# Four small edits to an encoder layer on one core: the attention planner's score cost, one copy's engine, the waits of the x rows, and the engine of one weight sum

## The chip, the cores and the metric

The kernel runs on one core of a Trainium2 chip. The metric is the device time of one execution in microseconds (us), from the first to the last instruction and what the launch adds around them.

## What is computed

One layer for 1024 prompt frames and 64 frames of a running stream: a half-step SwiGLU, two token mixers side by side (differential attention and retention) merged by gates, a second half-step SwiGLU, and a final norm. All of it is float32.

```python
x = x + 0.5 * g1 * swiglu(modulate(rms_norm(x, norm_f1), sh1, sc1), w_up1, w_down1)
hm = modulate(rms_norm(x, norm_mix), shm, scm)
q_a, k_a, v_a, q_r, k_r, v_r, z_r, gate_a, gate_r = split(hm @ w_in)
o_a = diff_attention(q_a, k_all, v_all)            # two softmaxes per head, a = p0 - lam * p1
o_r, s_new = retention(rotary(q_r), rotary(k_r), v_r, state)
o_a = head_rms_norm(o_a, da_norm) * (1 - lam_init)
o_r = head_group_norm(o_r, ret_norm) * silu(z_r)
merged = sigmoid(gate_a) * (o_a @ w_a_proj) + sigmoid(gate_r) * (o_r @ w_r_proj)
x = x + gm * (merged @ w_o)
x = x + 0.5 * g2 * swiglu(modulate(rms_norm(x, norm_f2), sh2, sc2), w_up2, w_down2)
y = rms_norm(x, norm_final)                        # shifts, scales and gates come from silu(c) @ w_ada + b_ada
```

The prompt's queries see earlier chunks of the prompt. The stream's 64 queries see a cache of 2048 keys and themselves.

## The kernel before

The 1088 columns (frames) are worked in two halves, g=0 (512 columns) and g=1 (576, the stream's 64 among them). Large products of a pair of weight blocks use a Strassen-like scheme (`pair_weights`, `products`, lines 520 to 554): seven products instead of eight. Each product is four blocks of three matmuls (`mm3`, lines 159 to 164), because every float32 operand is split into a high and a low part (`split`, line 132): ScalarE casts the high part (line 134), and VectorE or GpSimd subtracts it to get the low part (line 138).

For each pair of weight blocks `pair_weights` loads two raw tiles and makes four sums s1 to s4 (`add`, line 518). s2 needs s1, and s4 needs s2. Then it splits three tiles of sums and raw weights and one smaller one. `LOE` and `SE` say which engine makes each low part and each sum; `phase(i)` picks a row of them for each stage. Row 1 is that of the mixers. There are three buffers for such halves (NW = 3), so the weights of the next pair are made while the products of this one give buffers back.

The stages in order:

- First SwiGLU (`ffn`, line 565), g=0 then g=1. Beside the products of `up`, a side generator is advanced by a fixed number of steps (`pump`). At the start it runs `side_work` (line 808), which interleaves, by the string `PAT`, steps of the adaLN product (`ada`, "g"), yields ("y") and steps of `load_x(1, later)` ("r"). `load_x` takes g=1's x rows in five tiles: it issues a load into a single buffer, yields `WAIT` times, transposes the tile on TensorE, copies it with VectorE and ScalarE, and yields once more.
- Mixers (from line 859). Sums of squares of the last half (`sqa[1]`) are copied to another pool (line 862) for the norm of the next stage (lines 342 to 346). Then each half runs 20 pairs of products of w_in, that is 140 products. After each product `tick(g)` (line 968) gives the other tasks (attention, the stream's decode attention, retention) a budget of 2.0, of which each step takes its stated cost; a step yields its delay and its cost. `att_core` (line 1087) states the cost of a score step as 0.0034 x 128 for each block of 128 keys. When the pairs are done, the remaining tasks are run to their end (line 1399).
- Merge of the mixers (`project`, `add_out`), and the second SwiGLU with the final norm.

The order of instructions on each engine is then fixed by the compiling framework, which follows the program order and takes what it thinks is ready. At run time each engine is in order.

Of the kernel before, what the change touches and what calls it, by code (L numbers as in the profile page):

```python
# [34 lines left out]
DA, DB, DH, DR, DT, DX = 4, 1, 4, 2, 2, 2  # L35
UA = 12
DC, DK, DV, EARLY = 2, 2, 1, True
# [3 lines left out]
NB = len(BLK)  # L41
GRP = [(0, 512), (512, 576)]
BGRP = [[0, 1], [3, 2]]
NY, NV, NTT, SIDE0, SIDE, TAIL, SLACK, NRA, NS0, WAIT, NNEAR = 4, 2, 6, 7, 3, 2, 5, 3, 3, 1, 2
LOP = (1, 4)
NDG = 4
PAT = "gyry" * 8 + "g"
# [36 lines left out]
def encoder_layer(tc: tile.TileContext, a, o, stage=9):  # L84
    nc = tc.nc
# [10 lines left out]
    def close(*names):  # L96
        for name in names:
            guards.pop(name).__exit__(None, None, None)
# [27 lines left out]
    def misc():  # L126
        return psum["pool"].tile([P, 512], F32, tag="misc", name="misc", bufs=psum["misc"])
# [38 lines left out]
    V, G = nc.vector, nc.gpsimd  # L166
    LOE, SE = [], []
    LOES = [[G, V, V, V, G], [G, V, G, V, V], [G, V, V, G, G]]
    SES = [[G, G, G, G], [G, V, G, G], [V, V, G, G]]
    FE = [[V, V, G, G], [G, G, G, G], [V, V, V, G], [V, V, G, G]]  # L170

    def phase(i):
        LOE[:], SE[:] = LOES[i], SES[i]

# [659 lines left out]
    sqa = {}  # L834
# [24 lines left out]
    phase(1)  # L859
    upool = pool("u")  # L860
    sq1 = upool.tile([P, 576], F32, tag="ft", name="sq1", bufs=NFT)
    nc.vector.tensor_copy(sq1, sqa[1])
    close("n1", "x1", "ps_f1", "acc")
    mpool = pool("mix", "right")
    spsum = pool("ps_mix", space=PSUM)
# [19 lines left out]
    def c4():  # L885
        return dec["pool"].tile([P, dec["c4"]], F32, tag="c4", name="c4", bufs=NC4)

    def small(n=P):
        return mpool.tile([P, n], F32, tag=f"s{n}", name="s", bufs=6 if n == P else 4 if n > P else 2)

    def col(n=1):
        return mpool.tile([P, 8], F32, tag="col", name="col", bufs=24)[:, :n]
# [4 lines left out]
    def st():  # L897

        return dec["ps"].tile([P, dec["st"]], F32, tag="S", name="S", bufs=2048 // dec["st"])
# [65 lines left out]
    def spawn(gen, delay=1):  # L965
        tasks.append([now[0] + delay, gen])
# [103 lines left out]
    def heads_out(rows, ss, n, w, dcols, dst):  # L1070

        f = rsqrt(ss[:w, :n], 1.0 / VD)
        for j in range(n):
            nc.scalar.mul(rows[:, j], rows[:, j], f[:w, j:j + 1])
        yield DH, 0.1
        ot = c4()
        t = misc()
        for j in range(4):
            nc.tensor.transpose(t[:, j * w:(j + 1) * w], rows[:, j], ident[:w, :w])
        for j in range(0, 4, 1 if len(dcols) > 1 else 4):  # L1080
            e = (j + 1 if len(dcols) > 1 else 4) * w
            nc.scalar.mul(ot[:, j * w:e], t[:, j * w:e], dcols[j % len(dcols)])
        for q, (d, a0, a1) in enumerate(dst):
            nc.sync.dma_start(d, ot[:, a0:a1])
        yield 1, 0.9

    def att_core(g, h, q, ks, v, done):

        rows, ss = [], col(8)

        def scores(r):
            w = P * (4 * g + r + 1)
            p, sums = [], col(2)
            t = st()
            half = dec["st"] // 2
            both = t[:, :half], t[:, half:]
            for k, k0 in ks:
                k1 = min(k0 + 512, w)
                for c, s in enumerate(both):
                    cs = slice(c * HD, (c + 1) * HD)  # L1100
                    nc.tensor.matmul(s[:, k0:k1], q[cs, r * P:(r + 1) * P], k[cs, :k1 - k0], start=True, stop=True)
            for c, s in enumerate(both):
                nc.vector.memset(s[:HD, w - HD:w], -1e30)
                nm, sm = col(), sums[:, c:c + 1]
                nc.vector.tensor_reduce(out=nm, in_=s[:, :w], op=ALU.max, axis=AX.X, negate=True)
                e = c4()
                nc.scalar.activation(e[:, :w], s[:, :w], AF.Exp, bias=nm, accum_out=sm)
                p.append(e)
            rs, cf = col(2), col()
            nc.vector.reciprocal(rs, sums)  # L1110
            r0, r1 = rs[:, 0:1], rs[:, 1:2]
            nc.vector.scalar_tensor_tensor(out=cf, in0=sums[:, 0:1], scalar=r1, in1=neglam, op0=ALU.mult, op1=ALU.mult)
            nc.vector.scalar_tensor_tensor(out=p[0][:, :w], in0=p[1][:, :w], scalar=cf, in1=p[0][:, :w],
                                           op0=ALU.mult, op1=ALU.add)
            return p, r0

        def values(r, at, r0):
            if not rows:
                rows.append(mpool.tile([P, 4, P], F32, tag="rows", name="rows", bufs=1))
            n = 4 * g + r + 1  # L1120
            t = misc()
            for j in range(n):
                nc.tensor.matmul(t[:, :P], at[:, j * P:(j + 1) * P], v[j], start=(j == 0), stop=(j == n - 1))
            nc.scalar.mul(rows[0][:, r], t[:, :P], r0)
            nc.scalar.activation(small(), t[:, :P], AF.Square, scale=r0, accum_out=ss[:, r:r + 1])
            return 0.22 * n

        p, r0 = scores(0)
        yield DA, 0.0034 * 128 * (4 * g + 1)
        for r in range(4):  # L1130
            i = 4 * g + r
            at = p[1]
            for j0 in range(0, i + 1, 4):
                t = misc()
                n = min(4, i + 1 - j0)
                for j in range(n):
                    nc.tensor.transpose(t[:, j * P:(j + 1) * P], p[0][:, (j0 + j) * P:(j0 + j + 1) * P], ident)
                nc.scalar.copy(at[:, j0 * P:(j0 + n) * P], t[:, :n * P])
            yield DB, 0.22 * (i + 1)
            cur = r, at, r0  # L1140
            if r < 3 and EARLY:
                p, r0 = scores(r + 1)
                if r == 2:
                    done()
                yield DC, 0.0034 * 128 * (i + 2)
            cost = values(*cur)
            if r < 3 and not EARLY:
                p, r0 = scores(r + 1)
                if r == 2:
                    done()  # L1150
                cost += 0.0034 * 128 * (i + 2)
            yield DA - (DC if EARLY else 0), cost
        spawn(heads_out(rows[0], ss, 4, P, [dcol[:, h:h + 1]], [(osp_a[h][:, g * 512:g * 512 + 512], 0, 512)]))

# [183 lines left out]
    for g in range(2):  # L1338
# [9 lines left out]
        def attend():  # L1348
            for h in range(HEADS):
                yield from until(("q", h), ("v", h))  # L1350
                ks, vs = [(got["k", h], 512 * g)], [got["v", h][:, j] for j in range(4)]
                if g:
                    ks.insert(0, (kv(ksp[h]), 0))
                    va = kv(vsp[h]).rearrange("p (j c) -> p j c", c=P)
                    vs = [va[:, j] for j in range(4)] + vs
                    yield 3, 0.1
                yield from att_core(g, h, got["q", h], ks, vs, lambda: free("q", h))
                free("v", h)
# [25 lines left out]
        while lins or rest:  # L1384
            if lins and live[0] + lins[0][0] <= dec["u"]:
                n, f, i = lins.popleft()
# [120 lines left out]
    sqa = npool.tile([P, 576], F32, tag="yf", name="sqa", bufs=NY)  # L1507
# [97 lines left out]
```

## Time and profile before

| what | us |
|---|---|
| median of three runs | 2578.6 (2573.17 to 2580.3) |
| profiled execution, its own time | 2576.09 |
| its span, first to last instruction | 2574.3 |
| TensorE (PE) busy | 2446.7 (95%) |
| VectorE (DVE) busy | 1818.7 (71%) |
| GpSimd (POOL) busy | 1618.6 (63%) |
| ScalarE (ACT) busy | 1125.2 (44%) |

A busy PE is not always a PE at full speed: its matmuls overlap, and the granted clock falls at times. Stretches of the span have to be read one by one. Where PE sits idle, the view of waits says which instruction on which engine released it; that instruction may be late because its own engine, which is in order, was held by something else.

### The profile page before, as it was taken

To read this page: it belongs to the slowest core of one execution; us is meant where nothing else is said; L and a number is where in the kernel's file an instruction comes from. 1 tells how busy PE (TensorE), PEld (TensorE's weight loads), DVE (VectorE), ACT (ScalarE), POOL (GpSimd) and SP (SyncE) were. 2 spreads that over 40 slices of the span, in tenths; PEclk is the share of its full clock that TensorE was granted. 3 is DMA by queue.
4 is the path that set the end of the run, shared out by engine and by line. 5 is a ranking of instruction groups with operands and counts; after the bars stand their busy time and mean duration, and the time that the engine had idled before them with its cause. 6 is when DMAs were issued, how large, how long until landed. Compare 5 with 4: busy or idle time off the path is not lost. (4 is left out here: it accounts for less than half of the span.)

```text
span 2574.3 us, 45302 instructions
## 1 busy us (share of the span) xinstructions
PE 2446.7 (95%) x17278; PEld 2259.9 (88%) x17278; DVE 1818.7 (71%) x3132; ACT 1125.2 (44%) x1928; POOL 1618.6 (63%) x1058
## 2 busy tenths in 40 slices
PE   6999999999999889998999998999999999999998
PEld 3888889999999778887878986798889998999998
DVE  5586667776666897787665664557877777766766
ACT  4443335443334445553445545534444444333333
POOL 5796676887666466686444533655767665756562
PEclk9999999999999999999999998999999999999999
DMA  8655445554443553543333336646453335323331
GB/s 284 218 189 157 141 153 194 176 152 146 140 137 102 179 172 117 170 154 113 109 110 104 117 98 203 197 130 220 122 166 106 99 101 185 112 91 91 91 91 38
DMA packets 425005, 365.25 MB, mean 142 GB/s; under 512 B 18780, under 2 KB 358420, under 8 KB 424788
## 3 DMA queue, kind: packets, MB, share of 16 engines
q1 hardware_dynamic: 424608, 362.28, 45.3%
q8 instruction: 137, 2.24, 0.4%
q14 instruction: 80, 0.66, 0.1%
q10 hardware_dynamic: 180, 0.06, 0.0%
HBM read 307.95 MB, written 52.10 MB: 140 GB/s over the span
## 5 line engine op out<-in xcount | busy, mean ns | idle before, releaser
L162 PE MATMUL misc<-h,whi 128*128 128x288 f32 (+2 forms) x3360 | 1010.8, 301 | 32.8 <-DVE t L518 15.8
L164 PE MATMUL misc<-h,wlo 128*128 128x288 f32 (+2 forms) x3360 | 988.7, 295 | 9.7 <-DVE wlo L138 6.7
L163 PE MATMUL misc<-h,whi 128*128 128x288 f32 (+2 forms) x3360 | 990.0, 295 | 5.1 <-DVE h L138 5.0
L162 PEld LDWEIGHTS misc<-h,whi 128*128 128x128 f32 x3360 | 645.7, 192 | 72.4 <-DVE t L518 18.5
L164 PEld LDWEIGHTS misc<-h,wlo 128*128 128x128 f32 x3360 | 645.6, 192 | 16.4 <-DVE wlo L138 8.1
L163 PEld LDWEIGHTS misc<-h,whi 128*128 128x128 f32 x3360 | 645.8, 192 | 14.9 <-DVE h L138 7.1
L138 POOL TENSOR_TENSOR wlo<-raw,whi 128x1024 fp32r<-128x1024 f32 x150 | 374.7, 2498 | 270.3 <-ACT whi L134 236.2
L518 DVE TENSOR_TENSOR t<-misc,t 128x256 f32<-128x256 f32 (+1 forms) x560 | 235.0, 432 | 235.0 <-PE misc L164 202.0
L138 DVE TENSOR_TENSOR wlo<-ws,whi 128x1024 fp32r<-128x1024 f32 x178 | 313.5, 1761 | 62.4 <-ACT whi L134 61.1
L138 POOL TENSOR_TENSOR wd<-raw,wd 128x512 fp32r<-128x512 f32 x176 | 233.6, 1349 | 100.5 <-ACT wd L134 100.4
L653 DVE SCALAR_TENSOR_TENSOR x<-misc,gate,x 128x288 f32<-128x288 f32 (+3 forms) x540 | 239.8, 486 | 52.5 <-PE misc L164 45.1
L134 ACT CAST whi<-ws 128x1024 fp32r<-128x1024 f32 x178 | 186.7, 1049 | 203.6 <-PE misc L163 125.7
L134 ACT CAST whi<-raw 128x1024 fp32r<-128x1024 f32 x160 | 167.4, 1046 | 215.3 <-PE misc L163 170.8
L518 POOL TENSOR_TENSOR ws<-raw 128x512 f32<-128x512 f32 x134 | 192.4, 1438 | 98.9 <-DVE wlo L138 60.6
L134 ACT CAST wd<-raw 128x512 fp32r<-128x512 f32 x176 | 102.7, 619 | 186.9 <-PE misc L164 172.0
L162 PE MATMUL misc<-h,wd 128*128 128x288 f32 (+3 forms) x552 | 178.8, 327 | 5.1 <-DVE t L518 3.1
L163 PE MATMUL misc<-h,wd 128*128 128x288 f32 (+3 forms) x552 | 178.6, 325 | 0.0
L164 PE MATMUL misc<-h,wd 128*128 128x288 f32 (+3 forms) x552 | 176.4, 324 | 0.0
L518 POOL TENSOR_TENSOR h<-raw 128x512 f32<-128x512 f32 x78 | 109.7, 1407 | 84.1 <-issue 34.5
L162 PE MATMUL misc<-h,wb 128*128 128x256 f32 (+1 forms) x512 | 151.5, 296 | 5.2 <-ACT h L134 4.2
L163 PE MATMUL misc<-h,wb 128*128 128x256 f32 (+1 forms) x512 | 148.9, 291 | 0.0
L164 PE MATMUL misc<-h,wb 128*128 128x256 f32 (+1 forms) x512 | 148.9, 291 | 0.0
(297 smaller groups left out, 4787.2 us busy)
## 6 DMA issues: line engine op xcount, KB each, us to landing
raw<-in_w_up_dram SPq DMA_DIRECT2D x176, 512.0 KB, 4.0
raw<-in_w_down_dram SPq DMA_DIRECT2D x88, 512.0 KB, 4.0
raw<-in_w_in_dram SPq DMA_DIRECT2D x80, 512.0 KB, 4.0
rawa<-in_w_ada_dram SPq DMA_DIRECT2D x24, 1024.0 KB, 6.6
h<-in_w_ada_dram SPq DMA_DIRECT2D x16, 512.0 KB, 7.0
raw<-in_w_o_dram SPq DMA_DIRECT2D x16, 512.0 KB, 4.3
raw<-far SPq DMA_DIRECT2D x14, 576.0 KB, 3.7
yf<-xsp SPq DMA_DIRECT2D x24, 288.0 KB, 4.3
```

What stands on the lines that cost most here:

```text
L134: nc.scalar.copy(hi, src)
L138: eng.tensor_tensor(out=lo, in0=src, in1=hi.bitcast(F32), op=ALU.subtract)
L162: nc.tensor.matmul(out, wh, xh, start=first, stop=False)
L163: nc.tensor.matmul(out, wh, xl, start=False, stop=False)
L164: nc.tensor.matmul(out, wl, xh, start=False, stop=last)
L518: eng.tensor_tensor(out=out, in0=in0, in1=in1, op=op)
L653: nc.vector.scalar_tensor_tensor(out=xm, in0=t[:, c0 - cs.start:c1 - cs.start], scalar=gate()[:, m, s:s + 1], in1=xm, op0=ALU.mult, op1=AL ...
```

## The change

Four edits:

- `att_core` states the cost of a score step as 0.0018 x 128 for each block of 128 keys, in place of 0.0034 x 128, at all three places.
- The copy of the sums of squares (line 862) is made by ScalarE in place of VectorE.
- `WAIT` is 2 in place of 1: a yield more between the load of a tile of g=1's x rows and its transposes.
- In the mixers' row of `SES` the second of the four weight sums, s2 = s1 - a1, is made by GpSimd in place of VectorE, so that GpSimd makes all four.

```diff
-NY, NV, NTT, SIDE0, SIDE, TAIL, SLACK, NRA, NS0, WAIT, NNEAR = 4, 2, 6, 7, 3, 2, 5, 3, 3, 1, 2
+NY, NV, NTT, SIDE0, SIDE, TAIL, SLACK, NRA, NS0, WAIT, NNEAR = 4, 2, 6, 7, 3, 2, 5, 3, 3, 2, 2
...
-    SES = [[G, G, G, G], [G, V, G, G], [V, V, G, G]]
+    SES = [[G, G, G, G], [G, G, G, G], [V, V, G, G]]
...
-    nc.vector.tensor_copy(sq1, sqa[1])
+    nc.scalar.copy(sq1, sqa[1])
...
         p, r0 = scores(0)
-        yield DA, 0.0034 * 128 * (4 * g + 1)
+        yield DA, 0.0018 * 128 * (4 * g + 1)
...
-                yield DC, 0.0034 * 128 * (i + 2)
+                yield DC, 0.0018 * 128 * (i + 2)
...
-                cost += 0.0034 * 128 * (i + 2)
+                cost += 0.0018 * 128 * (i + 2)
```

## Rows read from the trace of the kernel before

**Rows 1.** The page's head and its busy times (us, share of span, instructions).

```profile
span 2574.3 us, 45302 instructions
PE 2446.7 (95%) x17278; PEld 2259.9 (88%) x17278; DVE 1818.7 (71%) x3132; ACT 1125.2 (44%) x1928; POOL 1618.6 (63%) x1058
```

**Rows 2.** Stretches (us): length, busy PE, PEld, DVE, ACT, POOL; clock, DMA, GB/s.

```profile
84.00:100.00 16.00, 12.38 (x84) 11.89 (x82) 6.16 (x15) 8.20 (x17) 9.34 (x7) 0.79 0.76 230
...
868.00:881.00 13.00, 8.68 (x43) 8.65 (x44) 12.97 (x20) 4.50 (x9) 10.61 (x8) 0.61 0.75 229
881.00:900.00 19.00, 16.03 (x131) 15.27 (x131) 16.44 (x29) 10.40 (x18) 12.91 (x8) 1.00 0.46 139
900.00:925.00 25.00, 20.34 (x128) 17.93 (x127) 23.42 (x50) 13.60 (x32) 14.31 (x9) 0.86 0.73 231
925.00:975.00 50.00, 45.21 (x347) 41.34 (x347) 43.41 (x94) 21.68 (x45) 32.95 (x23) 0.97 0.46 135
...
1098.00:1139.00 41.00, 37.41 (x311) 36.77 (x309) 34.49 (x48) 20.19 (x43) 30.33 (x18) 1.00 0.46 145
1139.00:1178.00 39.00, 31.47 (x213) 30.54 (x212) 34.21 (x34) 19.36 (x28) 34.11 (x18) 0.87 0.47 143
...
1558.70:1585.00 26.30, 16.55 (x119) 12.52 (x118) 13.78 (x40) 18.41 (x40) 10.66 (x12) 0.84 0.79 260
...
2250.00:2500.00 250.00, 250.00 (x1881) 250.00 (x1880) 177.14 (x360) 92.85 (x142) 151.38 (x101) 1.00 0.30 89
```

**Rows 3.** PE's waits, 857 to 975 us: releaser, us in total, times, longest.

```profile
PE misc L342 <- DVE sq L862: 4.5, 1, 4.5
PE misc L162 <- ACT u L952: 3.0, 1, 3.0
...
PE misc L162 <- DVE col L905: 1.8, 1, 1.8
```

**Rows 4.** DVE in order of time (start, us): the copy and three s2.

```profile
868.74 1.75 DVE L518 TENSOR_TENSOR h<-h,raw 128x512 f32<-128x512 f32 x1
...
871.08 1.19 DVE L862 COPY sq<-sqa 128x576 f32<-128x576 f32 x1
...
890.92 2.92 DVE L518 TENSOR_TENSOR h<-h,raw 128x512 f32<-128x512 f32 x1 [0.47 <-POOL h L518]
...
936.89 0.68 DVE L518 TENSOR_TENSOR h<-h,raw 128x512 f32<-128x512 f32 x1
...
960.24 2.86 DVE L518 TENSOR_TENSOR h<-h,raw 128x512 f32<-128x512 f32 x1
```

**Rows 5.** ACT in order of time: a cast of 576 columns.

```profile
846.87 0.67 ACT L134 CAST h<-v 128x576 fp32r<-128x576 f32 x1
```

**Rows 6.** POOL in order of time: two low parts of weights.

```profile
871.91 2.56 POOL L138 TENSOR_TENSOR wlo<-raw,whi 128x1024 fp32r<-128x1024 f32 x1
...
960.17 2.38 POOL L138 TENSOR_TENSOR wlo<-h,whi 128x1024 fp32r<-128x1024 f32 x1
```

**Rows 7.** Groups: s2 on DVE, s4 on POOL; busy us, mean ns, idle before.

```profile
L518 POOL TENSOR_TENSOR h<-raw,h 128x512 f32<-128x512 f32 x39 | 57.3, 1468 | 5.6 <-DVE h L518 5.6
L518 DVE TENSOR_TENSOR h<-h,raw 128x512 f32<-128x512 f32 x39 | 53.4, 1369 | 9.7 <-POOL h L518 9.6
```

**Rows 8.** PE's waits, 1135 to 1180 us.

```profile
PE misc L162 <- DVE t L518: 6.3, 2, 3.2
```

**Rows 9.** PE in order of time: decode work of the last head.

```profile
1558.74 3.68 PE L1204 MATMUL misc<-s,P 128*128 128x64 f32 x32
...
1566.22 1.91 PE L1212 MATMUL misc<-ck,c 128*64 128x128 f32 x16
```

**Rows 10.** PE's longest wait, 1560 to 1600 us.

```profile
PE misc L1315 <- DVE s L1305: 6.2, 1, 6.2
```

**Rows 11.** PE in order of time: transposes of the last two x tiles.

```profile
84.27 1.04 PE L742 MATMUL misc<-ident,xrow 128*128 128x128 f32 x8
...
92.36 1.08 PE L742 MATMUL misc<-ident,xrow 64*128 64x64 f32 x8 [3.62 <-DMA xrow<-in_x_sample_dram]
```

## The prediction

> **What bounds the kernel now.** I read the busy times first. PE is busy for 95% of the span, the next engine, DVE, for 71% [rows 1], so only time in which PE idles or runs slowly can be won. Then I cut the span into stretches [rows 2]. In the long steady one, 2250 to 2500 us, PE is busy for all 250 us at full clock: 1881 matmuls, 0.133 us each, so a product of twelve takes about 1.6 us. Nothing is to be won there, and the same holds for most of both SwiGLUs. The losses lie in a few short stretches, and these are where the four edits act: 84 to 100 us, where the x rows come in; 868 to 975, where the mixers begin; 1098 to 1178, the end of the mixers' first half; and 1558.7 to 1585, the end of the second half. In each I take two losses: idle time, which is length less busy time, and half clock, which is at most the length times one less the granted clock. 868 to 881 loses 4.3 us idle and up to 13 x 0.39 = 5.1 us by the clock. 881 to 975 loses 3.0 + 4.7 + 4.8 = 12.5 us idle, and 3.5 + 1.5 = 5 us by the clock. 1098 to 1178 loses 3.6 + 7.5 us idle and 5.1 by the clock. Last, I asked who released PE there [rows 3, 8, 10, 11]. From 868 to 975 DVE itself is the crowded engine: 13.0 of 13, 16.4 of 19, 23.4 of 25 and 43.4 of 50 us [rows 2].
>
> **The copy of the sums of squares.** PE waits 4.5 us for it, the longest wait of the stretch [rows 3]. It ends at 872.27. On DVE it stands behind an s2 of 1.75 us and takes 1.19 us itself [rows 4]. Both leave DVE. No copy of this shape on ACT is in the trace; the nearest row is a cast of 576 columns, 0.67 us [rows 5], and ACT is busy for only 4.5 of these 13 us [rows 2]. So the wait falls by 1.75 + (1.19 - 0.67) = 2.3 us. If the shorter idle time also spares half of the 5.1 us lost to the clock, the term is 2.3 + 2.5 = 4.8 us. There is a brake: the next pair's first low part, on POOL from 871.91 to 874.47 [rows 6], now stands behind one sum more (1.47 us [rows 7]) and is ready at about 875.9. PE has two products (24 matmuls, 3.2 us at full clock) of the old pair before it needs that, so the brake costs at most 1 us. I take -4. Bounds: 0, if ACT's copy lands behind a cast that waits for PE, and -7.
>
> **The weight sum s2.** 39 of them leave DVE (53.4 us, mean 1369 ns) and come to POOL. Of its four sums s4 is the one of the same shape and operands: 39 for 57.3 us, mean 1468 ns [rows 7]. Alone, an s2 takes DVE 0.68 us. The 2.86 us one at 960.24 begins with a 2.38 us low part on POOL and ends a little after it [rows 4, 6]: while POOL works on SBUF, this DVE instruction does not finish, and all of DVE's queue stands behind it. Ten of the 39 took over 2 us. So an s2 costs DVE between 0.68 and 2.9 us, and POOL about 1.5. On POOL it comes right behind s1, which it needs, so the hop to the other engine and back goes too. What stands behind it there is s3, s4 and the low parts; PE waits for these.
>
> At the mixers' beginning, 881 to 975, five s2 stand on DVE: 2.92, 0.68 and 2.86 us [rows 4], and two between them (1.30 and 1.69 us in the same view), 9.4 us together. The one at 890.92 stands ahead of the norm work that holds ACT, for which PE waits 3.0 us; the one at 960.24 is in the middle of the chain that ends in the 1.8 us wait for `col` [rows 3]. POOL has room: 60 of 94 us busy, and 5 x 1.47 = 7.3 more [rows 2]. Idle time and clock lose 17.5 us there. I take -5, which is about half of the DVE time taken away. Bounds: -12 (all of it, and the clock), and +2, if the added POOL time holds other DVE instructions as long as it frees them.
>
> From 1098 to 1139 there is little beside the products, and POOL is busy for 30.3 of 41 us; four sums add 5.9, which makes 36. It fits, but without slack; I take +1 (0 to +6, at 1.47 a sum). From 1139 to 1178 DVE and POOL are both full (34.2 and 34.1 of 39 us [rows 2]), and PE waits 6.3 us for DVE [rows 8]. Two s2 leave, 3.6 us; two come to POOL, 2.9, which makes 37 of 39. I take -1.5 (-8 to +5). In the second half POOL is under half busy, and most s2 take 0.7 us: -1 (-4 to +2). Together: -6.5.
>
> The Trainium skill speaks against this edit: the page "GPSIMD Engine Reference", section "4.1 Engine selection", sends two-input elementwise work on a tile to VectorE, as GpSimd takes about twice as long. This trace agrees for an s2 alone (0.68 against 1.47 us), not for the mean (1.37 against 1.47). By that rule the edit would be a loss; it is the second rival below.
>
> **The planner's cost.** I followed `tick` with the yields as they stand. In the first half a score step cost 0.44 to 1.74 of the 2.0 a tick, now 0.23 to 0.92. No step there moves: the delays bind, not the budget. In the second half it cost 2.18 to 3.48, so it used up its tick and left debts; now it costs 1.15 to 1.84 and lets one more step pass. The decode of the first head begins one tick earlier. The pair q1 comes at tick 35 of the half in place of 42, so the second head's scores and decode start 7 and 5 ticks earlier. The last head's decode ends at tick 144 in place of 150. The products end at tick 140 and retention at tick 148 in both. No work is added or removed. What moves is work of the last head from the tail, after the last product, to ahead of it: 34 matmuls of L1204 (3.68 us for 32) and half of the 32 of L1212 (1.91 us for 16) [rows 9], some 5.9 us. The tail, 1558.7 to 1585, has PE busy for 16.6 of 26.3 us [rows 2]; its longest wait, 6.2 us, is for retention's norm [rows 10], a chain of DVE, POOL and PE that this does not shorten. If that chain alone sets the tail, the moved work is paid twice: the tail stays and the part ahead of it grows by 5.9. If PE set it, nothing is lost. I take +4. Bounds: -4 (the steps spread better earlier on), and +9, as the second head now shares the score bank with three retention blocks more.
>
> **The wait of the x rows.** Before, the last tile (the stream's) is transposed two products after the one ahead of it: from 84.27 to 92.36, of which 3.62 us is PE's wait for the load [rows 11]; the clock loses up to 16 x 0.21 = 3.4 us [rows 2]. With a yield more per tile, five tiles take 15 steps and not 10. The fourth tile becomes the one with the short distance: three products after the third. The fifth falls into the next `up`, with long cover. 8.1 us from transposes to transposes, less 1.04 of their own and 3 x 1.6, leaves 2.3 us of idle in place of 3.6, so the stall moves more than it goes. The far sums behind it come five steps later, under the saturated products of the next two `up`. The fifth tile shares its buffer with a g tile of `up`, whose split now waits for the transposes; it is needed only two `up` later. I take -1.5. Bounds: -6.5 (wait and clock all gone) and +3, as the tile now in question is the larger one.
>
> **The sum.** -4 - 6.5 + 4 - 1.5 = -8.0 us on the profiled execution's 2576.1 us (2574.3 span): 2568.1. The median of the runs is 2.5 us above that execution, so the same change gives 2570.6, or 0.31% less than 2578.6.
>
> **Rivals.**
>
> One: the gains are swallowed. What is late next at 868 is the weights on POOL, and at 881 to 975 the chain PE, DVE, ACT that is long anyway; for it speaks that DVE stays over 80% busy after the relief. With half of the 9 us kept there and the tail paid in full (+5.9), the sum is near -1: about 2578. Against it: the waits of 4.5 and 3.0 us each have a moved instruction directly ahead of them.
>
> Two, the other side: POOL becomes what the products wait for in the first half. Its place is 975 to 1178 us, with 14 sums. The point from which it decides is where POOL's work per pair passes PE's: in 1139 to 1178 it is at 37 of 39 us by the count above. Each sum then delays the next low part by 1.47 - 0.68 = 0.8 us, 11 us in all, with no gain to set against it but the copy's: with the tail's +4, 2578.6 + 11 + 4 - 4 = 2590. For it speaks that POOL's low parts are also what holds DVE; against it, that POOL idles 10.7 us in 1098 to 1139 [rows 2].
>
> Three: the clock holds at the mixers' beginning, where short waits seem to bring most of the half clock. Then both terms there reach their far bounds, -7 and -12, and the sum is about -18: 2561.
>
> That an edit does nothing: the planner's may, in the first half; that is in the sum.
>
> **How the numbers follow.** Less than 0.3% (7.7 us) can hardly be told from no change here. Forecast 0.53, in its own range of 2563 to 2577: 0.36 of it beyond 0.3%, 0.17 within. Rival one 0.17, all within. Rival two 0.16: 0.15 slower. Rival three 0.10, faster. The rest, 0.04, is order on the engines that I don't foresee, split between slower and within. That gives 0.46 faster, 0.36 within, 0.18 slower. The range, with one in ten left out at either end, is 2557 to 2588.
>
> **What would show it.** The copy: an ACT instruction of about 0.7 us at L862, PE's wait at L342 at 2 to 2.5 us, clock over 0.61 after it. The sum: 39 more TENSOR_TENSOR on POOL, none of h<-h,raw on DVE, PE less idle from 881 to 975; wrong if new PE waits name POOL's wlo from 1098 to 1178. The planner: L1204 of the last head ahead of the last product, and a tail of about 26 us with more idle time; wrong if the tail shrinks by the 5.9 us. The x rows: a wait at L742 of about 2.3 us at a prompt tile. The prediction fails if the first 100 us of the mixers aren't shorter.

## The result, and the profile after

The changed kernel is slower: 2608.0 us (median of 4 runs, 2604.5 to 2612.7) against 2579.5 us (4 runs). The ratio is 1.0108, 95% interval 1.0088 to 1.0127, so +28 us (+23 to +33). The forecast was 2570.6 us, in a range of 2557 to 2588: the sign was wrong, and the range did not hold the result.

The head of its page, to be held against [rows 1]:

```profile
span 2607.0 us, 45279 instructions
PE 2453.2 (94%) x17278; PEld 2264.4 (87%) x17278; DVE 1798.8 (69%) x3092; ACT 1127.0 (43%) x1929; POOL 1674.1 (64%) x1097
```

The 39 sums did come to POOL (1058 instructions before, 1097 now; +55.5 us). But DVE, which gave up 53.4 us of s2 [rows 7] and a copy of 1.2 us, is busy for only 19.9 us less. More than half of the relief came back in other instructions. PE does the same 17278 matmuls in 33 us more of span.

To place the loss I aligned the traces by the columns that PE had streamed, and took for each stretch of the kernel before how much longer the same PE work took (us, one profiled execution each):

```
stretch of before   0-250  250-850  850-1000  1000-1300  1300-1400  1400-1525  1525-1650  1650-end
all four edits       12.3      1.4       8.5       -3.2        7.0        0.7        4.1       2.1
copy alone            2.7      1.9      -0.5        1.0       -0.1        0.0       -2.7       1.2
s2 alone              0.1      0.4       5.2       -4.3        0.3        1.5        1.0      -0.1
score cost alone      0.4     -0.5       1.5       -1.8        9.3        2.2        5.4      -0.7
wait alone           13.2      1.2       0.8       -1.8        1.0        0.0       -2.3       5.4
```

Up to 6 us in a cell can be chance (last section), so single cells are read together with the repeated runs, or over several traces. The large numbers lie where each edit acts: the x rows and what they push back, the start of the mixers, and two places in the mixers' second half.

The stretches of the changed kernel that answer to [rows 2] (length, busy PE, PEld, DVE, ACT, POOL; granted clock, DMA):

```profile
85.80:103.10 17.30, 12.15 (x76) 10.01 (x75) 9.25 (x16) 7.65 (x14) 8.42 (x7) 0.90 0.71 224
154.00:198.00 44.00, 37.92 (x247) 34.21 (x246) 34.45 (x56) 21.80 (x40) 32.09 (x24) 0.92 0.63 196
880.00:893.00 13.00, 9.47 (x67) 9.24 (x67) 11.84 (x20) 6.54 (x12) 12.31 (x9) 0.87 0.70 213
893.00:925.00 32.00, 25.25 (x172) 22.36 (x170) 23.77 (x48) 15.85 (x31) 18.53 (x12) 0.89 0.56 172
925.00:1000.00 75.00, 62.31 (x438) 56.94 (x439) 66.91 (x127) 30.34 (x65) 50.52 (x35) 0.89 0.48 141
...
1158.00:1198.00 40.00, 30.16 (x213) 28.34 (x212) 32.77 (x33) 19.10 (x28) 38.73 (x20) 0.91 0.45 141
1317.00:1420.00 103.00, 92.59 (x639) 78.91 (x637) 60.66 (x108) 45.42 (x91) 48.41 (x32) 0.97 0.33 99
...
1590.00:1617.00 27.00, 16.17 (x88) 10.73 (x89) 14.54 (x32) 16.29 (x36) 10.99 (x11) 0.73 0.80 250
```

In each of them PE idles, and the clock is below full speed too. From 925 to 1000 PE idles 12.7 us and up to 75 x 0.11 = 8.3 us go by the clock. The same PE work stood at 909 to 978 us in the kernel before; there (view 909 to 979) PE idled 9.5 us, and the clock of 0.95 took up to 3.5. POOL from 1158 to 1198 is busy for 38.7 of 40 us, close to the count in the prediction (37 of 39).

What PE waited for at the mixers' start in the changed kernel (us in all, times, longest), against [rows 3]:

```profile
PE misc L162 <- DVE t L518: 5.4, 4, 2.7
PE misc L162 <- ACT t L926: 4.9, 1, 4.9
PE misc L342 <- ACT sq L862: 3.5, 1, 3.5
```

The wait for the copy fell by 1.0 us, and the 3.0 us for `u` and 1.8 for `col` are gone from the top. A new one of 4.9 us stands in their place. Its cause is on DVE, in the second of the two products from which lambda, the weight of the second softmax, is made (L1056):

```profile
890.78 7.45 DVE L1056 TENSOR_TENSOR s<-s 128x64 f32<-128x64 f32 x1
```

and of POOL at the same time:

```profile
890.84 1.29 POOL L518 TENSOR_TENSOR h<-raw 128x512 f32<-128x512 f32 x1
892.10 2.40 POOL L138 TENSOR_TENSOR wlo<-h,whi 128x1024 fp32r<-128x1024 f32 x1
894.46 1.26 POOL L518 TENSOR_TENSOR h<-h,raw 128x512 f32<-128x512 f32 x1
895.68 1.25 POOL L518 TENSOR_TENSOR h<-raw 128x512 f32<-128x512 f32 x1
896.90 1.25 POOL L518 TENSOR_TENSOR h<-raw,h 128x512 f32<-128x512 f32 x1
```

A product of 64 columns takes 7.45 us: it begins 0.06 us ahead of five POOL instructions that run without a gap, and ends 0.08 us after the last. On ACT the table load for lambda's exponential (L1058) needs its result, and the copy `t` (L926) that PE waits for stands behind that:

```profile
898.56 1.28 ACT L1058 ACT_TABLE_LOAD   x1 [5.87 <-issue]
...
899.96 0.35 ACT L926 COPY t<-misc 128x256 f32<-128x256 f32 x1
```

Why the product did not get through between two of the five is not shown. In the kernel before, POOL also worked from 877.47 to 884.60 us without a gap over 0.1 us, and there the same product ended between two of its instructions:

```profile
878.69 2.92 DVE L1056 TENSOR_TENSOR s<-s 128x64 f32<-128x64 f32 x1
```

```profile
879.15 2.38 POOL L138 TENSOR_TENSOR wlo<-h,whi 128x1024 fp32r<-128x1024 f32 x1
881.61 1.29 POOL L518 TENSOR_TENSOR h<-raw 128x512 f32<-128x512 f32 x1
```

With s2 alone on POOL (e2 below) the two products took 0.78 and 0.22 us. So the long hold comes with the four edits together; s2 alone does not bring it.

### The profile page after: what moved, and what is told of

It is laid out like the page before. It is cut to its first block, busy times and chain, and to the rows that moved or that the text cites. A ratio compares the mean times of both kernels' runs of the same rounds, so it can differ in the third digit from the quotient of the medians.

```text
span 2607.0 us, 45279 instructions
## 1 busy us (share of the span) xinstructions
PE 2453.2 (94%) x17278; PEld 2264.4 (87%) x17278; DVE 1798.8 (69%) x3092; ACT 1127.0 (43%) x1929; POOL 1674.1 (64%) x1097
## 4 chain that ended last, share of the span: by engine, by line
PE 73%; DVE 11%; DMA 7%; issue 4%; ACT 2%; POOL 2%; SPq 1%; DVEq 0%; ACTq 0%; POOLq 0%
PE misc L162 20%; PE misc L163 19%; PE misc L164 19%; PE acc L162 2%; PE acc L163 2%; PE acc L164 2%; DVE wlo L138 2%; DVE h L138 1%; PE S L1101 1%; PE misc L1123 1%; PE misc L290 1%; DVE wb L138 1%; DMA far<-t 1%; DMA raw<-in_w_up_dram 1%; DMA rt<-u 1%
## 5 line engine op out<-in xcount | busy, mean ns | idle before, releaser
L162 PE MATMUL misc<-h,whi 128*128 128x288 f32 (+2 forms) x3360 | 1013.8, 302 | 33.2 <-DVE t L518 16.2
L138 POOL TENSOR_TENSOR wlo<-raw,whi 128x1024 fp32r<-128x1024 f32 x150 | 374.1, 2495 | 270.2 <-ACT whi L134 267.1
L138 DVE TENSOR_TENSOR wlo<-ws,whi 128x1024 fp32r<-128x1024 f32 x178 | 317.0, 1781 | 58.6 <-ACT whi L134 58.4
L138 POOL TENSOR_TENSOR wd<-raw,wd 128x512 fp32r<-128x512 f32 x176 | 235.1, 1358 | 116.5 <-ACT wd L134 116.5
L653 DVE SCALAR_TENSOR_TENSOR x<-misc,gate,x 128x288 f32<-128x288 f32 (+3 forms) x540 | 240.9, 487 | 65.2 <-PE misc L164 58.1
L162 PE MATMUL misc<-h,wd 128*128 128x288 f32 (+3 forms) x552 | 179.9, 329 | 10.3 <-DVE v L518 5.9
```

The costliest lines, as they stand in the source:

```text
L138: eng.tensor_tensor(out=lo, in0=src, in1=hi.bitcast(F32), op=ALU.subtract)
L162: nc.tensor.matmul(out, wh, xh, start=first, stop=False)
L653: nc.vector.scalar_tensor_tensor(out=xm, in0=t[:, c0 - cs.start:c1 - cs.start], scalar=gate()[:, m, s:s + 1], in1=xm, op0=ALU.mult, op1=AL ...
```

## Experiments

Differences are ratios times 2579 us, with the 95% interval of the ratio behind them.

**The four edits one at a time (e1 to e4), and all but s2 (e8).** Each is one line of the diff; e8 is the changed kernel with `[G, V, G, G]` put back.

> The copy on ScalarE alone. By place (where the two traces drift apart, PE's work aligned): from 850 to 890 us the changed kernel gains some 3 us against what it had lost before, so this edit alone should give -3 us (-5 to 0), with PE's wait for the copy down from 4.5 to about 3 us. By the prediction: -4. By the rival that only the four together reorder the engines and no part has a price of its own: within 2 us of zero, and the four parts' sum far from the +28 of the whole.

> s2 on GpSimd alone. By place: the changed kernel loses 7.4 us at 890 to 900 and 8.9 us at 930 to 950 (of the kernel before), gives back about 8 up to 1300. There GpSimd runs five instructions without a gap (890.8 to 898.2) and one small VectorE product of two SBUF tiles takes 7.45 us; so this edit alone: +6 to +13 us, most of it from 880 to 960, with single VectorE instructions over 5 us there. By the prediction: -6.5 us, waits from 881 to 975 shorter. By the rival of reordering alone: within 3 us of zero.

> The planner's cost alone. By place: the changed kernel loses 8 us between 1300 and 1370 and 5 us between 1540 and 1600 and nothing before 1240: so +5 to +12 us, all of it in the second half of the mixers. By the prediction: +4 us, in the tail's balance. By the rival that those two losses come from s2 on GpSimd as well (three more sums per pair's worth of waits): about 0, and e2 shows them.

> The x rows' wait alone. By place: the two traces are 12 us apart at 210 us and stay so until 850; nothing else differs there, so +11 to +13 us: 2 to 4 us from 80 to 150, 8 us at 172 to 190, where the far sums (five steps later) put eight VectorE instructions among the first down stage's. By the prediction: -1.5 us (to +3).

> The other three edits without s2 on GpSimd (s2 stays on VectorE). If the single prices add up (copy +3, cost +16, wait +14): +33 us, so s2 would be worth -5 in company. If s2's held VectorE instruction at 890 to 900 us costs what that place lost (7 us there and 7 at 930 to 950): +15 to +19 us. If s2 is worth the same as alone (+2): +26 us.

Measured: copy +2.8 us (0.0 to 5.7), s2 +2.3 (-1.0 to 5.9), cost +17.0 (13.2 to 20.9), wait +16.2 (12.1 to 20.4); all but s2 +27.1 (22.2 to 31.7). Cost and wait make the loss. s2 alone, and in company (28 less 27), is not told apart from nothing, where I expected 6 to 13 from the place; the copy does not gain. The single prices sum to 38, ten more than the whole; whether the edits overlap or the single runs read high stays open.

**The x rows.** The far sums (`far_sums`) follow the tiles in the same side generator: they norm g=1's x and make the sums that its products need. Four variants of the kernel before. e5 delays the far sums alone, e6 has the two waits but the far sums back in place, e10 brings the tiles late without more cover, e12 gives the second wait to the last tile only.

```diff
e5          yield from rows
+           for _ in range(5):
+               yield
            rms_cols(tiles(1, GRP), rcol[1])
e6   WAIT = 2, and in this call of far_sums
-           for _ in range(SLACK):
+           for _ in range(0):
e10             nc.sync.dma_start(xin[:, :, j * P:j * P + w], stage_x[0][:, :, :w])
+               yield
            yield
e12 -       for _ in range(WAIT):
    +       for _ in range(WAIT + (w < P)):
```

> The x rows as before (one yield), with five empty yields ahead of the far sums, so that only the far sums come five steps later. Theory 'late far sums' (their VectorE instructions now fall among those of the first down stage, where PE waits for v and t): +8 to +11 us, the loss at 172 to 190 us there, nothing from 75 to 125. Theory 'rows' (it is the tiles' own transposes and buffer that cost): at most +2 us.

> The converse: two yields for each tile of x rows, and the five yields of slack in these far sums taken out, so that the far sums stand where they stood before. Theory 'late far sums': +2 to +6 us are left, from 75 to 150 us (the tiles' own part), nothing at 172 to 190. Theory 'rows': the whole +12 to +16 us stays.

> One yield between load and transposes as before, but two yields behind each tile of x rows: the tiles come as late as with the change, their loads get no longer cover. Theory 'late tiles' (the fourth and fifth tile and the far sums fall into the time of the first down stage and share its raw buffers, ScalarE and VectorE): +9 to +15 us, as with the wait alone. Rival 'the longer hold of the load's buffer': +3 us or less.

> Two yields for the last tile of x rows alone (the stream's), whose load PE waited for 3.6 us. Theory 'late tiles': with one step more instead of five the lateness costs little and the wait of 3.6 us goes: -4 to +2 us. Rival 'rows' (a longer hold costs by itself): +3 us or more.

Measured: e5 +1.0 (-2.1 to 3.9), e6 +9.3 (5.4 to 12.9), e10 +6.4 (1.8 to 11.1), e12 -2.6 (-7.7 to 2.6). So the far sums alone are not it, against my theory. Late tiles without any more cover cost 6 of the 16; one step for the last tile alone costs nothing and gains nothing certain.

By place two losses can be told apart (aligned as above, us, one trace each):

```
stretch of before              0-125  125-150  150-190
wait alone (e4)                  5.7      0.0      8.1
far sums alone late (e5)        -2.3     -0.9      6.1
two waits, far sums back (e6)    6.2      4.1      2.6
tiles late, no more cover (e10)  1.9     -0.9      7.9
```

From 150 to 190 us the seven traces with late far sums (e4, e5, e10, the changed kernel, e8, e9, e16) lose 6.1 to 9.3, and the eleven others beside e6 -0.3 to 2.0. From 0 to 125 the six with two yields for every tile lose 3.4 to 6.2, the others -4.1 to 2.8. So the late far sums lose some 6 to 8 us where they land, and the tiles' own part is some 5. Yet e5 costs only 1 us as a whole, with some 2 or 3 won ahead of that place, and e5 and e6 sum to 10, not 16; why the two cost more together stays open.

And a stall like the one that the edit was to hide is there, in the trace of the wait alone (and, with 3.3 us, in the changed kernel, where the profile puts it down to DVE's L138). Its waits, 60 to 200 us:

```profile
PE misc L162 <- DVE v L518: 4.6, 2, 3.9
PE misc L742 <- DMA xrow<-in_x_prompt_dram: 3.5, 1, 3.5
```

Its fourth and fifth tile on PE, which before stood at 84.27 and 92.36 [rows 11]:

```profile
98.93 1.94 PE L742 MATMUL misc<-ident,xrow 128*128 128x128 f32 x8 [3.54 <-DMA xrow<-in_x_prompt_dram]
...
124.68 0.71 PE L742 MATMUL misc<-ident,xrow 64*128 64x64 f32 x8
```

And its DVE ahead of `v`, for which PE waits 3.9 us: steps of the far sums (L413, L405) among a down stage's updates (L653). The expectations call this down stage the first; by its updates, which begin at 110, 138 and 173 us in the kernel before, it is the third.

```profile
177.03 1.14 DVE L413 TENSOR_TENSOR t<-yf 128x288 f32<-128x288 f32 x1
178.09 0.42 DVE L518 TENSOR_TENSOR misc<-misc,t 128x256 f32<-128x256 f32 x1
178.43 0.73 DVE L653 SCALAR_TENSOR_TENSOR x<-acc,gate,x 128x512 f32<-128x512 f32 x1
179.09 0.62 DVE L413 TENSOR_TENSOR t<-yf,t 128x288 f32<-128x288 f32 x1
179.63 1.21 DVE L138 TENSOR_TENSOR wlo<-ws,whi 128x1024 fp32r<-128x1024 f32 x1
180.76 0.93 DVE L405 SCALAR_TENSOR_TENSOR yf<-yf,nc_norm_f,misc 128x512 f32<-128x512 f32 x2
181.61 0.74 DVE L653 SCALAR_TENSOR_TENSOR x<-acc,gate,x 128x512 f32<-128x512 f32 x1
```

`v` follows at 182.27, and PE goes on at 182.73.

**The planner's cost.** e7 and e11 keep 0.0018 and hold tasks of the second half back by ticks. e13 and e14 set the cost by head, e16 does so in company of the other three edits. (e13 has 0.0018 in the first half too; there PE's order is that of the kernel before.)

```diff
e7, e11   -  yield 3, 0.1                   # attend, g=1
          +  yield 10 if h == 1 else 3, 0.1
e11       -  yield 3, 0.1                   # att_decode, start
          +  yield 3 + (2, 7, 2, 6)[h], 0.1
e13, e16  +  0.0034 if g and h == 0 else 0.0018
e14       +  0.0018 if g and h == 0 else 0.0034
```

> The planner's cost at 0.0018, and head 1's attention of the second half held back by seven ticks, so that its scores stand at ticks 53 to 68 of the half as before, while the stream's decode stays as early as 0.0018 puts it. Theory 'scores meet retention' (head 1's scores at ticks 46 and 51 fall beside retention's blocks at 45, 49 and 54, which use the same score bank, and beside the first decode's long softmax): +2 to +6 us, against +16 with the cost alone, and the waits of L1137 and L1279 between 1340 and 1370 back at 2 to 3 us in all. Rival 'the earlier decode': +12 us or more stays.

> The planner's cost at 0.0018 with head 1's attention held by seven ticks, and the four decodes held by 2, 7, 2 and 6 ticks, so that attention, decode and retention stand within two ticks of their old places. Theory 'the earlier decode' (its long softmax and its products come where PE has least slack, and the tail is paid twice): 0 to +4 us. Rival (any other cost reorders the engines, whatever the ticks): +10 us or more.

> The planner's cost at 0.0018, but 0.0034 for head 0 of the second half. By a step-through of the planner this puts attention, retention and the first pairs back where they stood before; only the last three decodes are 2 to 6 ticks early. Theory 'head 0' (its scores, retention's blocks and the decode's steps each come a tick or two nearer to each other on the one score bank, ticks 30 to 60): the loss of 12 us from 1310 to 1380 is gone and the tail's 4 stays: +2 to +6 us. Rival 'decodes early': +10 us or more.

> The converse: 0.0018 for head 0 of the second half alone, 0.0034 elsewhere; the tail's ticks are those of before. Theory 'head 0': +9 to +14 us, all between 1310 and 1400. Rival 'decodes early': 0 to +5 us.

> All four edits, but head 0 of the second half at the old score cost. Theory 'head 0': the loss of 8 us between 1300 and 1370 goes, +17 to +22 us over the kernel before instead of +28. Rival: +26 to +30.

Measured: e7 +11.6 (7.2 to 16.0), e11 +17.5 (12.1 to 23.2), e13 +7.2 (4.1 to 10.6), e14 +12.1 (7.7 to 16.8), e16 +15.0 (10.6 to 19.1). Two theories fell: head 1's earlier scores (e7) and the earlier decodes (e11) don't explain it. (e11 has a loss of its own: besides 8.9 us at 1300 to 1400 it loses 11.7 at 1525 to 1650, where its held decodes end.) Head 0 does: its cost alone brings 12 us (e14), and taking it back brings all four edits from +28 to +15 (e16). In the alignment by PE's columns the seven traces with head 0 at the new cost lose 8.0 to 14.8 us at 1300 to 1400, the twelve others -1.2 to 0.9. The view of stretches (columns as above) for the same 95 us, 1300 to 1395, in five kernels. The kernel before:

```profile
1300.00:1395.00 95.00, 90.82 (x640) 77.67 (x640) 58.53 (x109) 44.30 (x91) 43.82 (x32) 1.00 0.35 104
```

Score cost alone (e3):

```profile
1300.00:1395.00 95.00, 85.36 (x567) 71.36 (x566) 50.89 (x99) 40.35 (x82) 36.03 (x26) 0.95 0.33 99
```

e7, head 1's attention held:

```profile
1300.00:1395.00 95.00, 88.29 (x572) 73.38 (x571) 53.52 (x96) 39.36 (x80) 38.60 (x26) 0.93 0.33 100
```

e13, head 0 at the old cost:

```profile
1300.00:1395.00 95.00, 91.69 (x641) 77.39 (x640) 59.83 (x115) 46.02 (x94) 41.97 (x31) 1.00 0.36 106
```

e14, head 0 alone at the new cost:

```profile
1300.00:1395.00 95.00, 85.73 (x540) 73.00 (x541) 53.49 (x102) 39.35 (x79) 37.30 (x26) 0.89 0.30 91
```

PE gets through 640 matmuls where head 0 has the old cost, 540 to 572 where it has the new one. Part of that is idle time (95 less busy PE: 5 us more than before in e3 and in e14), part the clock, at 0.95 and 0.89 in place of 1.00: up to 5 and 10 of the 95 us. What PE waits for is the softmax of the scores and the score bank (tile S: in the second half one buffer, which scores and retention share). PE's waits from 1300 to 1395 us in the kernel before (us in all, times, longest):

```profile
PE misc L1137 <- DVE c L1113: 1.5, 2, 0.9
PE S L1279 <- ACT c L1107: 1.0, 1, 1.0
```

in e3:

```profile
PE misc L1137 <- DVE c L1113: 4.7, 2, 4.1
PE S L1279 <- ACT c L1107: 2.8, 2, 2.1
```

and in e14:

```profile
PE S L1279 <- ACT c L1107: 4.9, 2, 2.9
PE misc L1137 <- DVE c L1113: 3.2, 3, 1.7
```

7.5 and 8.1 us, against 2.5 before and 1.0 in e13. In e7 the waits at L1279 are gone, as its theory had it, but those at L1137 are 6.7 us; so holding head 1 back moves the wait more than it ends it. L1279 is a block of retention that needs the bank that the scores hold until ACT has read them (L1107). So the old cost, too high as a price of PE time, did the work of a spacer. Which of the steps after head 0's scores needs the space stays open.

**s2 by place, and the held DVE.** e9 is the changed kernel with lambda's two products on POOL, so that the 7.45 us instruction leaves DVE; e17 and e18 are the kernel before with s2 on POOL for the pairs 8 to 19 or 0 to 7 of the first half only (the sums of pair 0 are made earlier, all on POOL, so e18 moves seven s2); e15 joins e12 and lambda's products on POOL.

```diff
e9, e15   -  nc.vector.tensor_tensor(out=lq[:, :HD], ... op=ALU.mult)
          +  nc.gpsimd.tensor_tensor(out=lq[:, :HD], ... op=ALU.mult)
e17, e18  +  SE[1] = nc.gpsimd if 8 <= turn[2] < 20 else nc.vector     # e18: turn[2] < 8
          +  turn[2] += 1
```

> All four edits, and the two small products for lambda (128x64, two SBUF tiles) made by GpSimd instead of VectorE. Theory 'held VectorE': the 7.45 us instruction is gone, the ScalarE copy and the product behind it come 5 to 7 us earlier, and the time is +21 to +24 us over the kernel before instead of +28. Rival (the stretch is late for another reason and waits elsewhere): +27 to +30, another wait in the same place.

> s2 on GpSimd for the pairs 8 to 19 of the first half alone (from about 990 us), on VectorE elsewhere. If gain and loss are real and cancel: -2 to -6 us, from 1000 to 1300. If both are chance: within 2 us of zero.

> The converse: s2 on GpSimd for the first eight pairs alone. If gain and loss are real and cancel: +4 to +8 us, from 850 to 1000. If both are chance: within 2 us of zero.

> The kernel before with two yields for the last tile of x rows alone and the two products for lambda on GpSimd. If both small gains are real (2 us, and 2 us of a VectorE instruction held for 2.9 us at 879): -2 to -6 us; if they are noise: 0.

Measured: e9 +23.7 (18.1 to 29.7), some 4 us less than all four edits, but within their interval; the 4.9 us wait for `t` is gone from its list. By place, the two traces in which that product takes 7.45 and 7.52 us (the changed kernel and e16) lose 4.6 and 4.5 us at 880 to 900, while e9, e2 and e18 win 2.4 to 2.8 there: the hold costs some 7 us in that stretch. e17 -0.5 (-4.1 to 3.4), e18 +6.7 (3.4 to 10.3): the loss at the start is clear of the noise, the gain later is not shown. The traces agree on the place of the loss: from 880 to 970 us the five with s2 on POOL there (e2, e18, the changed kernel, e9, e16) lose 5.8 to 11.3 us, the 14 others 0.4 to 4.5. In e18 seven s2 of 11.9 us in all left DVE, and DVE's busy time rose from 1818.7 to 1824.7 us. e15 +4.9 (2.1 to 8.0), where -2 to -6 was expected: two gains within noise did not add up, and why they cost is open. No variant beats the kernel before by more than its interval.

## Why the prediction was wrong

**The planner's cost: forecast +4 (-4 to +9), measured +17.** "What moves is work of the last head from the tail": that part fits, with 5.4 us at 1525 to 1650 in e3 for the 5.9 paid twice. e13, in which only later decodes move, costs 7.2, of which its trace shows 4.0 there. What failed is "it costs ... and lets one more step pass", taken as free elsewhere. The second head on the score bank was named, but only as an upper bound of 5 us beside the 4, and the first head not at all. 9 to 12 us lie there (e3 by place, e14 by its runs).

**The wait of the x rows: forecast -1.5 (-6.5 to +3), measured +16.** The fourth tile's wait was foreseen, but with 2.3 us; it is 3.5, as long as the one that it replaced. The fifth tile does have cover: PE does not wait for it (124.68). The step that failed is the far sums "five steps later, under the saturated products of the next two `up`", at no price. From the fourth `up` on the generator gets 3 steps an `up` in place of 7 (`SIDE`, `SIDE0`), so five steps are some 35 to 40 us: the far sums stand from 161 to 210 us in place of 125 to 171. That carries them into the third down stage, where PE waits 3.9 us for `v` behind them; 6 to 8 us lie there, some 5 with the tiles. Before, they stood in the second down stage, and PE waited 1.9 us in all from 100 to 215. Why the third bears them worse stays open. I had looked at whether the products keep PE full, not at whether the engines beside them have room.

**s2: forecast -6.5, measured +2.3 (-1.0 to 5.9), and +6.7 for the first eight pairs.** The mechanism was read rightly (an s2 of 0.68 us alone took 2.86 beside a low part of 2.38 us on POOL) and priced in one direction only. The failed step is "about half of the DVE time taken away" as a gain: in e2 53.4 us of s2 leave DVE and its busy time falls by 22.8. The rest of the hold does not leave with s2: it passes to other such instructions in DVE's queue. The upper bound of +2 named this, and was too near. The page "GPSIMD Engine Reference" of the Trainium skill, section "4.1 Engine selection", advises against such work on GpSimd as about twice as slow; that agrees with the sign of this result: 1.47 us on POOL for 0.68 on DVE alone, no gain in e2 and a loss in e18.

**The copy: forecast -4, measured +2.8 (0.0 to 5.7).** On ACT it takes 0.67 us as taken from the cast, but the wait fell only from 4.5 to 3.8 in e1, where the copy's input, the last sum of squares, still stands behind an s2 on DVE. In the changed kernel that s2 is gone from DVE too, and the wait fell only to 3.5, where 2.3 us less was forecast: the last two sums of squares take 2.59 us there beside POOL's sums (881.05), against 0.41 for one in e1. So the step that failed is the 1.75 us for s2, which other held instructions of DVE take up. In e1:

```profile
PE misc L342 <- ACT sq L862: 3.8, 1, 3.8
```

```profile
873.23 1.74 DVE L518 TENSOR_TENSOR h<-h,raw 128x512 f32<-128x512 f32 x1
874.90 0.41 DVE L334 TENSOR_TENSOR sqa<-sqa,sq 128x256 f32<-128x256 f32 x1
```

And ACT is in order too:

```profile
875.40 0.67 ACT L862 COPY sq<-sqa 128x576 f32<-128x576 f32 x1 [3.72 <-DVE sqa L334]
875.98 1.04 ACT L134 CAST whi<-raw 128x1024 fp32r<-128x1024 f32 x1
```

The copy waits at the head of ACT, and the first pair's cast stands behind it; before, that cast (867.12) began some 4 us ahead of DVE's copy. I had bounded the case that the copy lands behind a cast, not the cast behind the copy. What the later cast costs is not shown: e1's trace loses nothing from 850 to 1000.

**The sum and the rivals.** Of +28 us, wait and cost make nearly all, and no rival named them. The rival on the slower side named POOL from 975 to 1178, and there the traces lose nothing. The clock entered the sum only as a gain where waits go; it has a price where waits come too, up to as much again as the added idle time in e3 (5 us by a clock of 0.95) and twice that in e14 (10 us by 0.89).

## What to carry to other kernels

A planner's cost is also a spacer: before a cost is made true, ask which chain on other engines the wrong cost kept apart. A step that is pushed back is to be priced by the room on every engine where it lands. An instruction moved off an engine that another one holds frees that engine only if its neighbours in the queue are not held in turn.

## What the runs showed of the hardware

A 128x64 product of two SBUF tiles on DVE, the second of lambda's, took 0.22 us in e2 and 2.92 us beside one low part on POOL in the kernel before. Beside five POOL instructions without a gap it took 7.45 us in the changed kernel, and 7.52 us in e16.

The same order of instructions can differ by some 5 us of time in one place. In e13 the order on all four engines is that of the kernel before up to 1300 us, yet 850 to 1000 takes 6.4 us longer. In e14 and e11, of that order too, it takes 6.3 and 4.2 us longer, in e3 and e7 1.6 and 1.1. DVE waits for a transfer there, before:

```profile
970.56 0.43 DVE L1240 TENSOR_TENSOR u<-u,rt 128x256 f32<-128x256 f32 x1 [0.74 <-DMA rt<-u]
```

and in e13:

```profile
973.56 0.42 DVE L1240 TENSOR_TENSOR u<-u,rt 128x256 f32<-128x256 f32 x1 [2.54 <-DMA rt<-u]
```

The transfer comes 1.8 us later against the work before it, and PE loses some 5 us behind that: it waits 2.5 us at L948 (975.24), and the granted clock is 0.83 from 968 to 998, against 0.93 for 965 to 990 before. A difference of this size in one trace is not evidence; the intervals of the repeated runs are.
